# Attention head pairs with two block products between their transposes and the last blocks in one PSUM bank; final rows written in groups of 3, 1, 3, 1

## The chip, the cores and the metric

The kernel runs on one core of one Trainium2 chip. The metric is the device time of one execution in microseconds, the median of several runs: 2482.18 us before the change (three runs, 2481.7 to 2482.43). The engines are named as in the profile: PE is TensorE (PEld its weight loads), DVE is VectorE, ACT is ScalarE, POOL is GpSimd, SP is SyncE, which here only issues DMAs.

## What is computed

A two-layer encoder trunk in fp32 over 640 tokens: 512 frames of a new stream (the prompt) and 8 running streams of 16 frames each (the samples), with a model width of 1024. Cut to what matters:

```python
for l in range(DEPTH):                                    # DEPTH = 2
    x = x + 0.5 * swiglu(rmsnorm(x, norm_ffn1[l]), ...)   # width 2816
    z = rmsnorm(x, norm_mix[l]) @ w_in[l]                 # conv B | C | V | q | k | v | gates
    y_conv = B * causal_conv3(C * V)                      # 512 channels
    s = q @ k.T * 64 ** -0.5 + rel_bias[clipped distance] # 8 heads x 64, chunk-banded mask
    y_attn = softmax(s) @ v
    x = x + (sig(g_c) * (y_conv @ w_conv_out) + sig(g_a) * (y_attn @ w_attn_out)) @ w_o
    x = x + 0.5 * swiglu(rmsnorm(x, norm_ffn2[l]), ...)
y = rmsnorm(x, norm_final)                                # 640 x 1024
```

New keys, values and convolution states are outputs too. The change touches two places: the prompt's `softmax(s) @ v`, and the final norm.

## The kernel before

**Layout.** Activations lie transposed, with channels on the 128 partitions: `x[k]` is channels 128k to 128k+127 by 640 tokens. Weights stream from DRAM in slabs of 128 x 1024 (`raw`, loaded by SP at L245). Every fp32 operand is split in two parts (ACT casts the high part at L305, DVE subtracts for the low part at L310), and each product is three PE matmuls (high x high, high x low, low x high).

**Block products.** The large products use a seven-product scheme on halves of 320 tokens. `seven` (L818) is a generator: for one pair of output rows it issues seven products in the order 11, 21, N6, T5, T7, 22, T4, each in two steps of 6 matmuls of 128x320 (`block`, L386), so 14 steps to a pair of rows. Banks `ma` (11, N6, T7, T4), `mb` (21) and `mc` (T5, then 22) hold the sums. Between two products into the same bank an engine has to read the bank: after T5, ACT copies `mc` to `c` (L848) before 22 may go on accumulating there; after N6, ACT copies `ma` (L844) before T7; after T7, DVE adds `ma` and `c` (L249) before T4.

**Attention.** For the prompt the 8 heads go in 4 pairs. `scores(p)` makes q times k for 128-row blocks of queries and keys (`pss`) and reduces them on DVE (L1805); ACT takes exponentials (L1969) and scales the rows (L1816). `values(p)` transposes the weights block by block on PE (`ptp`, L1829). For key block j there are 4-j blocks of 128 for each of the two heads e, one PSUM bank for each j and e. Each bank is then copied to SBUF (`pt`, L1832), and the product with the values follows (`py`, L1843: 8 matmuls of 64 rows, two for each j, shown as 16 records), which ACT copies out (L1845). PE executes in the order of the code here (it alone is ordered by hand in this stage; DVE and ACT instructions are placed by a scheduler, with the copies at raised priority). Between these parts `fill(n)` lets PE do n steps of the running block products, so that the other engines have time to finish what PE needs next. Before the change a pair is: 14 transposes (j = 0 and 1), 3 steps, 6 transposes (j = 2 and 3), 2 steps, `py`, 5 steps; pairs 0 to 2 have the scores of the next pair and 4 more steps ahead. For pairs 0 to 2 this comes to: transposes, T5, half of T7, transposes, the other half of T7 and half of 22, `py`, half of 22, T4 and 11 of the next pair of rows. In pair 3 it is: transposes, 21 and half of N6, transposes, half of N6 and half of T5, `py`, and so on.

**Banks.** The transposes, scores and `py` share a pool of four PSUM banks (`att`) in turn, so a bank's new user waits until its last user has been read.

**The end.** `Final.all` (L2013 to L2066) adds the last part of the second FFN to `x` and applies the final norm, in two parts of the tokens: A (the first 384) and B (the last 256). While PE makes B's products, DVE multiplies A's rows by the norm factor `frr` (L2112), two of the eight `x[k]` at a time, and SP writes them to `yout` (L2113): rows 0-1, 2-3 and 4-5 behind B's rows 5, 6 and 7, and rows 6-7 after B's norm factors have been put on a diagonal (L488), while PE spreads them over the partitions (`nbcf`, L2103). Then DVE scales B's eight rows (L2116), and SP and ACT in turn write each as a DMA of 128 KB (L2118).

Of the kernel before, what the change touches and what calls it, by code (L numbers as in the profile page):

```python
# [13 lines left out]
ALU = mybir.AluOpType  # L14
PSUM = bass.MemoryType.PSUM

P = 128
# [30 lines left out]
PARTS = slice(0, 3 * P), slice(3 * P, T)  # L48
# [132 lines left out]
def trunk(ctx: ExitStack, tc: tile.TileContext, xin, xtok, wst, small, pbias, samplebias, kcache, vcache,  # L181
          yout, ko, vo, co):
    nc = tc.nc
    PE, DVE, ACT, POOL, SP = nc.tensor, nc.vector, nc.scalar, nc.gpsimd, nc.sync
# [21 lines left out]
    def acc(name):  # L206
        return banks["acc"].tile([P, 2, 512], F32, tag="acc", name=name)

    def att(name):
        return banks["att"].tile([P, 512], F32, tag="att", name=name)  # L210
# [15 lines left out]
    for kind, inside in kinds():  # L226
        n = len(fourth)
# [20 lines left out]
    def add(out, a, b):  # L248
        DVE.tensor_tensor(out=out, in0=a, in1=b, op=ALU.add)  # L249
# [58 lines left out]
    def flush():  # L308
        for lo, src, hi in pending:
            DVE.tensor_tensor(out=lo, in0=src, in1=hi.bitcast(F32), op=ALU.subtract)  # L310
        pending.clear()
# [3 lines left out]
    def slab(hold=False):  # L315

        flush()
        i = used[0]
        used[0] += 1
        while len(ready) < min(i + 2, len(slabs)):  # L320
            prep(len(ready))
            flush()
        prep(i + 2)
        if not hold:
            flush()
        return ready[i], slabs[i]
# [19 lines left out]
    class Tiles:  # L346
# [6 lines left out]
        def take(self):  # L353
            if self.at == self.n:
                self.cur, (kind, _, width) = slab(hold[0])
                assert kind == "plain"
                self.at, self.n = 0, width // P
            j = self.at
            self.at += 1
            return tuple(c[:, j * P : (j + 1) * P] for c in self.cur)  # L360
# [4 lines left out]
    def soon():  # L365
        return tc.high_priority(offset=300)
# [42 lines left out]
    def stir(ps, n):  # L409
        for _ in range(n):  # L410
            PE.matmul(ps[:, :P], ones, ones, start=True, stop=True)
# [4 lines left out]
    xall = xp.tile([P, KT, T], F32, name="x")  # L416
# [48 lines left out]
    class Stats:  # L465
# [19 lines left out]
        def turn(self, out, r):  # L485

            n = out.shape[1] // P
            DVE.tensor_tensor(out=out.rearrange("p (c t) -> p c t", c=n),  # L488
                              in0=ident.unsqueeze(1).to_broadcast([P, n, P]),
                              in1=r.unsqueeze(2).to_broadcast([P, n, P]), op=ALU.mult)  # L490

    def scaled(out, ps, rr):
        DVE.tensor_tensor(out=halves(out), in0=two(ps), in1=halves(rr), op=ALU.mult)
# [121 lines left out]
    def opening(fp, name, goff, n, put, tails):  # L615
# [45 lines left out]
        def out(i):  # L661

            j, up = divmod(i, 2)
            if not up:
                gs.append(tmp(f"g{name}_{j}"))
                if j:
                    scaled(gs[j], ps[i], ex.rho)
                    ACT.activation(gs[j], gs[j], AF.Silu)
                else:
                    ACT.copy(halves(gs[j]), two(ps[i]))  # L670
                return
            u = tmp(f"u{name}_{j}") if j > 1 else fp.tile([P, T], F32, tag="cap", name=f"u{name}_{j}", bufs=5)
            us.append(u)
            if j:
                scaled(u, ps[i], ex.rho)
                DVE.tensor_tensor(out=u, in0=u, in1=gs[j], op=ALU.mult)
            else:
                ACT.copy(halves(u), two(ps[i]))
# [559 lines left out]
    def mixer(l, after):  # L1238
        with tc.tile_pool(name=f"yp{l}", bufs=1, reuse_waits="tile") as yp, \
# [19 lines left out]
            with tc.tile_pool(name=f"mp{l}", bufs=2, reuse_waits="tile") as mp:  # L1259
# [63 lines left out]
                with tc.manual_schedule(engines={mybir.EngineType.PE}):  # L1323
                    attention(l, h, st, stats, ops, mp, yas, ycp, both, others())
# [374 lines left out]
    def attention(l, h, norms, stats, ops, mp, yas, ycp, both, others):  # L1699


        rr = norms.rr
        npair = H // 2
        nt = T // P
        NQ = SEQ // P
# [30 lines left out]
        def fill(n):  # L1736
            for _ in range(n):
                next(stream, None)
# [80 lines left out]
        def values(p):  # L1819

            pt = [mp.tile([P, offs[-1] + SEQ], F32, name=f"pt{l}_{2 * p + e}", tag="pt") for e in range(2)]
            at = [sum(P * (NQ - i) for i in range(j)) for j in range(NQ)]

            def turn(j, e):
                w = (NQ - j) * P
                s = weights[2 * p + e]
                ptp = att(f"ptp{l}_{2 * p + e}_{j}")[:, :w]
                for i in range(j, NQ):
                    PE.transpose(ptp[:, (i - j) * P : (i - j + 1) * P],  # L1829
                                 s[:, offs[i] + j * P : offs[i] + (j + 1) * P], ident)  # L1830
                with soon():
                    (ACT.copy if e and j % 2 else DVE.tensor_copy)(pt[e][:, at[j] : at[j] + w], ptp)  # L1832

            for j in range(NQ):
                for e in range(2):
                    turn(j, e)
                if j % 2:
                    yield
            py = att(f"py{l}_{p}")
            for j in range(NQ):  # L1840
                for e in range(2):
                    hh = 2 * p + e
                    PE.matmul(py[e * HD : (e + 1) * HD, j * P :], vs[j][:, hh * HD : (hh + 1) * HD],  # L1843
                              pt[e][:, at[j] : at[j] + (NQ - j) * P], start=j == 0, stop=j == NQ - 1)
            ACT.copy(yas[:, p, 0:SEQ], py)  # L1845
            yield
# [5 lines left out]
        for p in range(npair):  # L1852
            if p + 1 < npair:
                scores(p + 1)
                fill(4)
            vals = values(p)
            next(vals)
            fill(3)
            next(vals)
            fill(2)  # L1860
            next(vals)
            fill(5)


        sbias = mp.tile([P, KS], F32, name=f"sbias{l}", bufs=1)
# [143 lines left out]
    class Final:  # L2009
# [8 lines left out]
        def all(self, ops):  # L2018
            ws = [[tiles.take() for _ in ops] for m in range(KT)]
            flush()  # L2020
            rr = pool[0].tile([P, PARTS[0].stop], F32, tag="even", name="frr", bufs=1)
            A, B = PARTS

            ACT.activation(early, x[KT - 1][:, 0:1], AF.Sqrt, bias=epst[:, 0:1], scale=0.0)
            for m in range(KT):
                self.product(0, m, ops, ws[m])
                self.take(0, m, m < KT - 1)
                if m:
                    self.scale(m - 1)
            for m in range(KT):  # L2030
                self.product(1, m, ops, ws[m])
                if m == 2:
                    self.ps = att("npsf0")[:, : A.stop // P]
                    for b in range(A.stop // P):
                        PE.matmul(self.ps[:, b : b + 1], self.ssum[0][:, b * P : (b + 1) * P], ones[:, 0:1],
                                  start=True, stop=True)
                    self.root(0)
                if m == 3:
                    self.turn(0)
                    self.scale(KT - 1)  # L2040
                if m == 4:
                    ps = self.spread(0)
                if m == 5:
                    self.ps = acc("npsf1")[:, :, 0]
                    self.idle = acc("stirf")[:, 0]
                    self.add(self.ssum[1], True)
                if m > 4:
                    self.add(self.sq)
                if m == 0:
                    last = self.sq  # L2050
                self.take(1, m, m < 4)
                if m == 0:
                    add(self.ssum[0], self.ssum[0], last)
                if m == 4:
                    ACT.copy(rr, ps)
                if m > 4:
                    self.two(2 * m - 10, rr)
            stir(self.idle, 3)
            self.add(self.sq, False, True)
            stir(self.idle, 5)  # L2060
            self.root(1)
            self.turn(1)
            self.two(6, rr)
            ps = self.spread(1)
            for k in range(KT):
                self.out(k, B, ps)  # L2066
# [40 lines left out]
            xk = x[k][:, PARTS[0]]  # L2107
            ACT.activation(xk, xk, AF.Copy, scale=sm[:, O_GF + k : O_GF + k + 1])

        def two(self, k, rr):  # L2110
            z = xall[:, k : k + 2, PARTS[0]]
            DVE.tensor_tensor(out=z, in0=z, in1=rr.unsqueeze(1).to_broadcast([P, 2, rr.shape[1]]), op=ALU.mult)  # L2112
            SP.dma_start(yout[:, k : k + 2, PARTS[0]], z)  # L2113

        def out(self, k, c, ps):
            DVE.scalar_tensor_tensor(out=x[k][:, c], in0=x[k][:, c], scalar=sm[:, O_GF + k : O_GF + k + 1],  # L2116
# [167 lines left out]
```

## Time and profile before

| | |
|---|---|
| median of three runs | 2482.18 us |
| the profiled execution's own time | 2482.18 us |
| its span, first to last instruction | 2480.2 us |
| mean granted TensorE clock | 0.999 |
| PE busy | 2469.0 us |
| DVE busy | 2119.5 us |
| ACT busy | 1442.9 us |
| POOL busy | 361.1 us |
| DMA, mean over the span | 125 GB/s |

All times in the rows are microseconds from the start of the span. A row of the timeline has the start, the duration, the engine, the line, the operation, the tiles (out<-in), the shape and a count of merged instructions; in square brackets stands how long the engine was idle before it and what released it. The profiled execution took 1.98 us more than its span, and its time is that of the median run.

### The profile page before, as it was taken

Reading aid. Unit: us, or ns where it says so; the run is one execution under the profiler, and the core shown is the slowest. Engines: PE = TensorE matmul, PEld = TensorE weight load, DVE = VectorE, ACT = ScalarE, POOL = GpSimd, SP = SyncE. Lnnn points to the kernel's source line nnn. Section 1 sums busy time; section 2 is a strip of 40 time slices with the busy share of each in tenths; the row PEclk is TensorE's granted clock in tenths of the full one; section 3 lists DMA queues with packets and bytes.
Section 4 is the critical chain, followed back from the end, with each engine's and each line's share of the span. In section 5 each row is a group of like instructions: output and inputs, shape, how many; then the busy total and the mean of one; then the engine's idle time right before and its main releaser. Section 6 shows DMA issues by size and latency. Waiting matters only on the chain.

```text
span 2480.2 us, 43569 instructions
## 1 busy us (share of the span) xinstructions
PE 2469.0 (100%) x17070; PEld 2422.0 (98%) x17070; DVE 2119.5 (85%) x3344; ACT 1442.9 (58%) x2337; POOL 361.1 (15%) x445
## 2 busy tenths in 40 slices
PE   9999999999999999999999999999999999999998
PEld 9999999889999999999999999998899999999998
DVE  7789888878888899888798889888788888989887
ACT  6445556665666555555565555556656665555555
POOL 0011211210111011111001111221101210111111
PEclk9999999999999999999999999999999999999999
DMA  5245665335345345555435454643344553555554
GB/s 189 82 115 125 136 136 130 107 111 175 104 112 153 95 117 121 133 136 136 117 92 129 129 132 123 138 120 110 122 156 123 119 140 92 122 131 124 129 136 111
DMA packets 134925, 310.72 MB, mean 125 GB/s; under 512 B 12896, under 2 KB 76768, under 8 KB 134720
## 3 DMA queue, kind: packets, MB, share of 16 engines
q1 hardware_dynamic: 70640, 221.80, 27.2%
q0 software_dynamic: 63360, 85.50, 20.7%
q8 instruction: 133, 2.18, 0.4%
q10 hardware_dynamic: 720, 0.65, 0.1%
q14 instruction: 72, 0.59, 0.1%
HBM read 223.75 MB, written 7.94 MB: 93 GB/s over the span
## 4 chain that ended last, share of the span: by engine, by line
PE 96%; ACT 2%; DVE 1%; DMA 0%; issue 0%; DVEq 0%
PE pab L395 12%; PE paa L395 11%; PE pcb L395 6%; PE pca L395 6%; PE dab L1086 5%; PE daa L1086 5%; PE qa L395 4%; PE po L372 4%; PE pbb L395 3%; PE pba L395 3%; PE dcb L1086 3%; PE dca L1086 3%; PE pda L372 2%; PE pv L1752 2%; PE poa L372 2%; PE ma_cv L395 2%
## 5 line engine op out<-in xcount | busy, mean ns | idle before, releaser
L310 DVE TENSOR_TENSOR wlo<-raw,whi 128x1024 fp32r<-128x1024 f32 (+1 forms) x582 | 597.4, 1030 | 243.2 <-ACT whi L305 240.1
L305 ACT CAST whi<-raw 128x1024 fp32r<-128x1024 f32 (+1 forms) x582 | 520.3, 896 | 359.2 <-PE pbb L395 39.4
L305 ACT CAST whi<-s 128x1024 fp32r<-128x1024 f32 (+1 forms) x164 | 153.4, 936 | 243.9 <-issue 109.1
L395 PE MATMUL pab<-xhib,whi 128*128 128x320 f32 x704 | 217.8, 309 | 0.0
L395 PE MATMUL pab<-xlob,whi 128*128 128x320 f32 x704 | 217.4, 309 | 0.0
L395 PE MATMUL pab<-xhib,wlo 128*128 128x320 f32 x704 | 217.4, 309 | 0.0
L395 PE MATMUL paa<-xhia,whi 128*128 128x320 f32 x640 | 197.9, 309 | 0.0
L395 PE MATMUL paa<-xhia,wlo 128*128 128x320 f32 x640 | 197.7, 309 | 0.0
L395 PE MATMUL paa<-xloa,whi 128*128 128x320 f32 x640 | 197.7, 309 | 0.0
L310 DVE TENSOR_TENSOR wlo<-s,whi 128x1024 fp32r<-128x1024 f32 (+1 forms) x164 | 176.3, 1075 | 6.4 <-ACT whi L305 6.1
L395 PEld LDWEIGHTS pab<-xhib,whi 128*128 128x128 f32 x704 | 132.2, 188 | 0.2
L395 PEld LDWEIGHTS pab<-xlob,whi 128*128 128x128 f32 x704 | 132.2, 188 | 0.2
L395 PEld LDWEIGHTS pab<-xhib,wlo 128*128 128x128 f32 x704 | 132.2, 188 | 0.0
L395 PEld LDWEIGHTS paa<-xloa,whi 128*128 128x128 f32 x640 | 120.2, 188 | 0.1
L395 PEld LDWEIGHTS paa<-xhia,whi 128*128 128x128 f32 x640 | 120.2, 188 | 0.1
L395 PEld LDWEIGHTS paa<-xhia,wlo 128*128 128x128 f32 x640 | 120.2, 188 | 0.0
L249 DVE TENSOR_TENSOR raw<-raw,raw 128x512 f32<-128x512 f32 x164 | 112.0, 683 | 1.2
L249 DVE TENSOR_TENSOR raw<-s,raw 128x512 f32<-128x512 f32 x164 | 111.9, 682 | 0.0
L395 PE MATMUL pcb<-xhib,whi 128*128 128x320 f32 x352 | 108.9, 309 | 0.0
L395 PE MATMUL pcb<-xlob,whi 128*128 128x320 f32 x352 | 108.7, 309 | 0.0
L395 PE MATMUL pcb<-xhib,wlo 128*128 128x320 f32 x352 | 108.7, 309 | 0.0
L1110 POOL DMA_DIRECT2D x<-c_b x52 | 62.6, 1203 | 310.4 <-ACT c_b L1103 104.1
(852 smaller groups left out, 8144.9 us busy)
## 6 DMA issues: line engine op xcount, KB each, us to landing
raw<-in_wst SPq DMA_DIRECT2D x374, 512.0 KB, 3.6
x<-c_b POOLq DMA_DIRECT2D x52, 320.0 KB, 5.1
x<-c_a POOLq DMA_DIRECT2D x50, 320.0 KB, 5.0
kc<-in_kcache SPq DMA_DIRECT2D x32, 256.0 KB, 3.7
vc<-in_vcache SPq DMA_DIRECT2D x16, 512.0 KB, 5.5
ub<-cbb POOLq DMA_DIRECT2D x42, 160.0 KB, 5.9
ua<-cba POOLq DMA_DIRECT2D x38, 160.0 KB, 5.5
x<-u_a POOLq DMA_DIRECT2D x18, 320.0 KB, 5.1
```

The lines of the kernel that those rows point to most:

```text
L249: DVE.tensor_tensor(out=out, in0=a, in1=b, op=ALU.add)
L305: ACT.copy(hi[:, d], src[:, c])
L310: DVE.tensor_tensor(out=lo, in0=src, in1=hi.bitcast(F32), op=ALU.subtract)
L372: PE.matmul(ps[a] if isinstance(ps, list) else ps[:, a, :HT], w, x[:, a * HT : (a + 1) * HT], start=first and j == 0, stop=last and j == 2)
L395: PE.matmul(ps, a, b, start=start and kp == 0 and j == 0, stop=stop and kp == NP - 1 and j == 2, skip_group_check=True)
L1086: PE.matmul(ps[u], w, y, start=start and i == 0 and j == 0, stop=i == 1 and j == 2, skip_group_check=True)
L1110: POOL.dma_start(rows(r, cols), z, accum_op=ALU.add)
L1752: PE.matmul(pv[t], xx[:, t * P : (t + 1) * P], w[:, kk * AW : (kk + 1) * AW], start=c == 0 and kk == 0 and j == 0, stop=c == KT // 2 - 1 a ...
```

## The change

In `values(p)`: one bank still takes one j and e for j = 0, 1 and 2, but for j = 3 the single blocks of both heads share one bank. Of the copies from the banks, DVE now takes j = 0 and 1 of both heads, and j = 2 and 3 of the first; ACT takes j = 2 and 3 of the second (before: j = 1 and 3 of the second). The steps around them go from 3, 2, 5 to 2, 2, 6, the same sum: for pairs 0 to 2 the order is now transposes, T5, transposes, T7, `py`, 22, T4, 11; for pair 3 transposes, 21, transposes, N6, `py`, T5. In `Final`, A's rows are scaled and written as 0-2, 3, 4-6 and 7.

```diff
             for j in range(NQ):
+                ptps = [att(f"ptp{l}_{2 * p + e}_{j}") for e in range(2 if j < NQ - 1 else 1)]
+                if j == NQ - 1:
+                    ptps = [ptps[0][:, e * P : (e + 1) * P] for e in range(2)]
                 for e in range(2):
-                    turn(j, e)
+                    turn(ptps[e], j, e)
+                    if j < NQ - 1:
+                        take(ptps[e], j, e)
+                if j == NQ - 1:
+                    for e in range(2):
+                        take(ptps[e], j, e)
                 if j % 2:
                     yield
...
+            def take(ptp, j, e):
+                w = (NQ - j) * P
                 with soon():
-                    (ACT.copy if e and j % 2 else DVE.tensor_copy)(pt[e][:, at[j] : at[j] + w], ptp)
+                    (ACT.copy if e and j > 1 else DVE.tensor_copy)(pt[e][:, at[j] : at[j] + w], ptp[:, :w])
...
             next(vals)
-            fill(3)
+            fill(2)
             next(vals)
             fill(2)
             next(vals)
-            fill(5)
+            fill(6)
...
                 if m > 4:
-                    self.two(2 * m - 10, rr)
+                    self.rows(*((0, 3), (3, 1), (4, 3))[m - 5], rr)
...
             self.turn(1)
-            self.two(6, rr)
+            self.rows(7, 1, rr)
...
-        def two(self, k, rr):
-            z = xall[:, k : k + 2, PARTS[0]]
-            DVE.tensor_tensor(out=z, in0=z, in1=rr.unsqueeze(1).to_broadcast([P, 2, rr.shape[1]]), op=ALU.mult)
-            SP.dma_start(yout[:, k : k + 2, PARTS[0]], z)
+        def rows(self, k, n, rr):
+            z = xall[:, k : k + n, PARTS[0]]
+            DVE.tensor_tensor(out=z, in0=z, in1=rr.unsqueeze(1).to_broadcast([P, n, rr.shape[1]]), op=ALU.mult)
+            SP.dma_start(yout[:, k : k + n, PARTS[0]], z)
```

What this does to the order of the instructions, at three places. The first is PE in layer 0, pair 0, around `py`. Names end in a number of the tile; `ma_qk_5261<-thi` is product T7 and `mc_qk_5382<-hhim` or `<-hlom` product 22. Before:

```order
L395 MATMUL ma_qk_5261<-thi_3_4696,whi_5257 128x320
L395 MATMUL ma_qk_5261<-tlo_3_4697,whi_5257 128x320
L395 MATMUL ma_qk_5261<-thi_3_4696,wlo_5258 128x320
L395 MATMUL mc_qk_5382<-hhim_1_4635,whi_5257 128x320
L395 MATMUL mc_qk_5382<-hlom_1_4636,whi_5257 128x320
L395 MATMUL mc_qk_5382<-hhim_1_4635,wlo_5258 128x320
L395 MATMUL mc_qk_5382<-hhim_3_4643,whi_5257 128x320
L395 MATMUL mc_qk_5382<-hlom_3_4644,whi_5257 128x320
L395 MATMUL mc_qk_5382<-hhim_3_4643,wlo_5258 128x320
L1843 MATMUL py_0_5436<-pt_0_5357,v_0_4887 64x512
L1843 MATMUL py_0_5436<-pt_1_5358,v_0_4887 64x512
L1843 MATMUL py_0_5436<-pt_0_5357,v_1_4888 64x384
```

And after (lines behind the edit in `values` stand 9 further down, so L1852 is what L1843 was):

```order
L395 MATMUL ma_qk_5261<-thi_3_4696,whi_5257 128x320
L395 MATMUL ma_qk_5261<-tlo_3_4697,whi_5257 128x320
L395 MATMUL ma_qk_5261<-thi_3_4696,wlo_5258 128x320
L1852 MATMUL py_0_5427<-pt_0_5357,v_0_4887 64x512
L1852 MATMUL py_0_5427<-pt_1_5358,v_0_4887 64x512
L1852 MATMUL py_0_5427<-pt_0_5357,v_1_4888 64x384
L1852 MATMUL py_0_5427<-pt_1_5358,v_1_4888 64x384
L1852 MATMUL py_0_5427<-pt_0_5357,v_2_4889 64x256
L1852 MATMUL py_0_5427<-pt_1_5358,v_2_4889 64x256
L1852 MATMUL py_0_5427<-pt_0_5357,v_3_4890 64x128
L1852 MATMUL py_0_5427<-pt_1_5358,v_3_4890 64x128
L395 MATMUL mc_qk_5382<-hhim_1_4635,whi_5257 128x320
```

Before, half of T7 and the first half of 22 (which begins with the `mc_qk` rows shown) stood between the last transposes and `py`; now the whole of T7 stands there, and the whole of 22 behind `py`.

The second place is ACT in the same pair. L844 copies `ma` after N6, L848 copies `mc` after T5, L305 casts a slab of weights, L1969 and L1816 belong to the softmax of the next head, and L1832 copies banks of transposes. Before:

```order
L844 COPY capsm_4687<-ma_qk_5261 128x320
L1969 ACTIVATE s_3_5282,st_3_5283<-s_3_5282,st_3_5283 128x128
L1969 ACTIVATE s_3_5282,st_3_5283<-s_3_5282,st_3_5283 128x256
L1832 COPY pt_1_5358<-ptp_1_1_5376 128x384
L1816 ACTIVATE s_2_5277<-s_2_5277,st_2_5278 128x128
L1816 ACTIVATE s_2_5277<-s_2_5277,st_2_5278 128x256
L1816 ACTIVATE s_2_5277<-s_2_5277,st_2_5278 128x384
L305 CAST whi_5398<-raw_5396 128x1024
L848 COPY c_4698<-mc_qk_5382 128x320
L1816 ACTIVATE s_2_5277<-s_2_5277,st_2_5278 128x512
L1832 COPY pt_1_5358<-ptp_1_3_5419 128x128
```

And after (L1978 is what L1969 was; `ptp_0_3_5403` is the bank that both heads share for j = 3):

```order
L844 COPY capsm_4687<-ma_qk_5261 128x320
L1978 ACTIVATE s_3_5282,st_3_5283<-s_3_5282,st_3_5283 128x128
L1978 ACTIVATE s_3_5282,st_3_5283<-s_3_5282,st_3_5283 128x256
L1816 ACTIVATE s_2_5277<-s_2_5277,st_2_5278 128x128
L1816 ACTIVATE s_2_5277<-s_2_5277,st_2_5278 128x256
L1816 ACTIVATE s_2_5277<-s_2_5277,st_2_5278 128x384
L1816 ACTIVATE s_2_5277<-s_2_5277,st_2_5278 128x512
L848 COPY c_4698<-mc_qk_5382 128x320
L305 CAST whi_5411<-raw_5409 128x1024
L1833 COPY pt_1_5358<-ptp_1_2_5396 128x256
L1833 COPY pt_1_5358<-ptp_0_3_5403 128x128
```

The copy of 384 is gone from ACT, a copy of 256 has come behind the cast, and the copy of `mc` (L848), which stood right behind the cast of 1024, now stands right ahead of it. In the same stretch DVE now has all its copies of the pair (512, 512, 384, 384, 256 and 128 columns) ahead of its subtraction for that slab (L310), where its copies for j = 2 and 3 stood behind it. In each layer SP issues one weight slab (`raw`, L245) behind the two loads of the value cache (`vc`) of samples 0 and 1 instead of ahead of them. POOL's order is the same.

The third place is DVE at the end of the program. L2078 adds B's products to `x`, L2112 scales A's rows, L2098 and L488 make B's norm factors, L2116 scales B's rows. Before:

```order
L2078 SCALAR_TENSOR_TENSOR x<-pdf_5_27190,x 128x256
L2112 TENSOR_TENSOR x<-x,frr 128x2x384
L2078 SCALAR_TENSOR_TENSOR x<-pdf_6_27208,x 128x256
L2112 TENSOR_TENSOR x<-x,frr 128x2x384
L2078 SCALAR_TENSOR_TENSOR x<-pdf_7_27222,x 128x256
L2112 TENSOR_TENSOR x<-x,frr 128x2x384
L2098 RECIPROCAL ninvf<-nrmsf 128x2
L488 TENSOR_TENSOR fsum_27031<-ident,ninvf 128x256
L2112 TENSOR_TENSOR x<-x,frr 128x2x384
L2116 SCALAR_TENSOR_TENSOR x<-x,sm,nbcf_27251 128x256 x8
```

And after (numbers of lines 9 higher):

```order
L2087 SCALAR_TENSOR_TENSOR x<-pdf_5_27182,x 128x256
L2121 TENSOR_TENSOR x<-x,frr 128x3x384
L2087 SCALAR_TENSOR_TENSOR x<-pdf_6_27200,x 128x256
L2121 TENSOR_TENSOR x<-x,frr 128x384
L2087 SCALAR_TENSOR_TENSOR x<-pdf_7_27214,x 128x256
L2121 TENSOR_TENSOR x<-x,frr 128x3x384
L2107 RECIPROCAL ninvf<-nrmsf 128x2
L488 TENSOR_TENSOR fsum_27023<-ident,ninvf 128x256
L2121 TENSOR_TENSOR x<-x,frr 128x384
L2125 SCALAR_TENSOR_TENSOR x<-x,sm,nbcf_27243 128x256 x8
```

The order is the same; the four scalings now take 3, 1, 3 and 1 rows of `x` instead of 2 each. The rest of the program is unchanged.

More of the change, by code (lines that the diff above doesn't have):

```diff
@@ L1822, in values, with turn @@
             at = [sum(P * (NQ - i) for i in range(j)) for j in range(NQ)]
-            def turn(j, e):
-                w = (NQ - j) * P
+            def turn(ptp, j, e):
                 s = weights[2 * p + e]
-                ptp = att(f"ptp{l}_{2 * p + e}_{j}")[:, :w]
                 for i in range(j, NQ):
```

## The prediction

> **What bounds the kernel now.** I read the page first. Its head and the list of engines:
>
> ```profile
> span 2480.2 us, 43569 instructions
> PE 2469.0 (100%) x17070; PEld 2422.0 (98%) x17070; DVE 2119.5 (85%) x3344; ACT 1442.9 (58%) x2337; POOL 361.1 (15%) x445
> ```
>
> PE leaves 11.2 us of 2480.2 unused, and part of that is the end, when only the output is still moving. Neither part of the change takes work from PE, so it can gain in two ways only: where PE stands still, or behind PE's last matmul. Who makes PE stand still is in the waits of PE; the columns are the waiter, the engine waited for, total us, times and the longest:
>
> ```profile
> PE mc_qk L395 <- ACT c L848: 1.6, 4, 0.4
> ...
> PE mc_cv L395 <- ACT c L848: 0.8, 2, 0.4
> ```
>
> Six waits, one line: the first matmul of product 22 waits until ACT has copied `mc` after T5. By their places they are pairs 0, 1 and 2 of both layers; pair 3 has none. I went to the first in the timeline of PE:
>
> ```profile
> 494.64 0.31 PE L395 MATMUL ma_qk<-thi,whi 128*128 128x320 f32 x1
> ...
> 495.53 0.82 PE L1829 MATMUL ptp<-ident,yc 128*128 128x128 f32 x6
> 496.10 0.40 PE L395 MATMUL ma_qk<-thi,whi 128*128 128x320 f32 x1
> ...
> 496.92 0.31 PE L395 MATMUL ma_qk<-thi,wlo 128*128 128x320 f32 x1
> 497.63 0.42 PE L395 MATMUL mc_qk<-hhim,whi 128*128 128x320 f32 x1 [0.40 <-ACT c L848]
> 497.89 0.31 PE L395 MATMUL mc_qk<-hlom,whi 128*128 128x320 f32 x1
> ...
> 498.71 2.38 PE L1843 MATMUL py<-pt,v 128*64 128x512 f32 x16
> 501.01 0.42 PE L395 MATMUL mc_qk<-hhim,whi 128*128 128x320 f32 x1
> ```
>
> Ends are modelled and overlap, so I count from start to start. Six matmuls of T7 take 495.53 - 494.64 = 0.89 us, 0.148 each. From T7's last matmul (496.92) to the second of 22 (497.89) are 0.97 us where two steps, 0.30, would do: **0.67 us lost**, not the 0.40 in the bracket. The last of the six:
>
> ```profile
> 1764.78 0.31 PE L395 MATMUL ma_cv<-thi,wlo 128*128 128x320 f32 x1
> 1765.52 0.41 PE L395 MATMUL mc_cv<-hhim,whi 128*128 128x320 f32 x1 [0.43 <-ACT c L848]
> 1765.77 0.30 PE L395 MATMUL mc_cv<-hlom,whi 128*128 128x320 f32 x1
> ```
>
> 0.99 - 0.30 = 0.69 us. Six by 0.68 are **4.1 us**. By the waits' own totals, 1.6 + 0.8, they are 2.4 us, which I keep as the lower end. Why the copy is late stands in ACT's timeline:
>
> ```profile
> 494.65 0.46 ACT L1832 COPY pt<-ptp 128x384 f32<-128x384 f32 x1
> 495.01 1.31 ACT L1816 ACTIVATE s<-s,st 128x128 f32<-128x128 f32 x3
> 496.22 1.04 ACT L305 CAST whi<-raw 128x1024 fp32r<-128x1024 f32 x1
> 497.16 0.42 ACT L848 COPY c<-mc_qk 128x320 f32<-128x320 f32 x1
> 497.47 0.73 ACT L1816 ACTIVATE s<-s,st 128x512 f32<-128x512 f32 x1
> 498.10 0.25 ACT L1832 COPY pt<-ptp 128x128 f32<-128x128 f32 x1
> ```
>
> No row waits: ACT is a queue here, and the copy stands behind a copy of 384, three scalings and a cast.
>
> **The pairs, step by step.** *PE.* The transposes, T7 and `py` change places; the numbers of matmuls and of passages from one kind to another are the same, so the work costs nothing more. After: six transposes from 494.64 take 496.10 - 495.53 = 0.57, to 495.21. T7 whole is 0.97 (496.10 to 496.92 and one step) and 0.89, to 497.07. `py` takes 501.01 - 498.71 = 2.30, to 499.37, and only then comes 22: 2.3 us later than the 497.07 at which it wanted to start.
>
> *ACT.* The 384 copy goes (0.36 from start to start). From 494.65: three scalings 1.21, the scaling of 512, which now stands ahead, 0.63, to 496.49; then the copy of `mc`, 0.42, done at 496.91. 22 wants it at 499.37: 2.5 us to spare. The six waits go: **-4.1 us**. Either half would have done in pair 0: with ACT's old order, `c` at 497.58 is still ahead of 499.37.
>
> *What is late next.* First, the banks. The last transposes start 0.89 us earlier and reuse the banks of the first ones. DVE's rows there:
>
> ```profile
> 492.81 0.68 DVE L1832 COPY pt<-ptp 128x512 f32<-128x512 f32 x1
> 493.58 0.18 DVE L1972 RECIPROCAL st<-st 128x4 f32<-128x4 f32 x1
> 493.68 1.12 DVE L1832 COPY pt<-ptp 128x512 f32<-128x512 f32 x2
> 497.30 1.23 DVE L310 TENSOR_TENSOR wlo<-raw,whi 128x1024 fp32r<-128x1024 f32 x1 [2.50 <-ACT whi L305]
> ```
>
> The first bank has been read at 493.49 and the next two at 494.80. The shared bank for j = 3 reuses the third, and PE comes to it after four transposes, at 494.64 + 4 x 0.095 = 495.02: 0.2 us to spare. Second, `py`. DVE has 2.5 us idle ahead of its subtraction, where its further copies now go (384, 256, 128; net 128 columns more than before), so `py` finds them. Of head 1, j = 2 comes from ACT: behind `c` (done 496.91; ACT goes on at about 496.80, since 497.16 to 497.47 is 0.31) the cast takes 0.94, to 497.74, the 256 copy at most the 384's 0.46, to 498.20. `py` reaches j = 2 after 1792 of 2560 columns, 497.07 + 0.70 x 2.30 = 498.68: 0.5 us to spare.
>
> A third point is the bank shared for j = 3: the transposes of both heads have to be in before either copy, and DVE's and ACT's copies go one after the other, one ACT row of 0.25 later. `py` reads j = 3 last, after 90% of its columns, so I cost it at nothing. The Trainium skill ("PSUM — Partial Sum Buffer", "PSUM bank collisions raise a hardware error") says that two engines, two readers among them, may not be on one bank and partitions at once, and that this must be guarded by bank; no run here shows it. By that rule both copies would be kept apart even though they read other columns, and it speaks against the shared bank; the sum stays as it is, as it is made with the copies apart.
>
> *SP.* Its one moved load stands behind two loads of the value cache. In layer 0 SP's row with the issue, and ACT's with the first use:
>
> ```profile
> 550.73 0.33 SPq L245 DMA_DIRECT2D raw<-in_wst  x1
> ```
>
> ```profile
> 570.27 1.05 ACT L305 CAST whi<-raw 128x1024 fp32r<-128x1024 f32 x1 [1.18 <-PE mc_b L395]
> ```
>
> 19.5 us lie between them, so a few us later cost nothing; without this cover PE would wait for that slab, by what the issue comes later.
>
> **The end.** DVE's rows there, of which the last eight are B's:
>
> ```profile
> 2467.46 0.95 DVE L2112 TENSOR_TENSOR x<-x,frr 128x768 f32<-128x768 f32 x1
> 2468.73 0.42 DVE L2078 SCALAR_TENSOR_TENSOR x<-pdf,x 128x256 f32<-128x256 f32 x1 [0.32 <-PE pdf L2073]
> ...
> 2470.27 0.95 DVE L2112 TENSOR_TENSOR x<-x,frr 128x768 f32<-128x768 f32 x1
> 2471.86 0.17 DVE L2098 RECIPROCAL ninvf<-nrmsf 128x2 f32<-128x2 f32 x1 [0.64 <-ACT nrmsf L2093]
> ...
> 2472.40 0.95 DVE L2112 TENSOR_TENSOR x<-x,frr 128x768 f32<-128x768 f32 x1
> 2473.28 3.22 DVE L2116 SCALAR_TENSOR_TENSOR x<-x,sm,nbcf 128x256 f32<-128x256 f32 x8
> ```
>
> 256 columns take 0.42 and 768 take 0.95, so 384 take some 0.55 and 1152 some 1.35. Three rows from 2467.46 end at 2468.81, 0.08 behind the add that PE releases at 2468.73; three from 2470.27 end at 2471.62, ahead of the reciprocal at 2471.86. The chain to B's scaling is not longer, and the 0.08 goes in the second scaling, which is 0.40 shorter. I leave the start of B's scaling (2473.28) where it is. What moves is the bytes. The DMA rate over 2468 to 2480 in 40 slices of 0.3 us:
>
> ```profile
> GB/s 0 0 0 0 164 358 384 353 51 5 348 374 364 225 343 364 379 220 0 0 0 333 343 399 338 341 341 324 355 335 341 352 335 331 324 14 0 0 0 0
> ```
>
> The first data move half way into slice 4, at 2469.36, 0.95 us after the scaling's end (2468.41). From slice 21 (2474.30) to 2478.51 the DMA engines run without a gap at some 342 GB/s: 0.39 MB of rows 6 and 7 and 1.05 MB of B. Three empty slices (18 to 20) lie ahead of this burst. After the change rows 4 to 6 (0.59 MB) are scaled at 2471.62 and move from 2472.57 to 2474.30; row 7 (0.20 MB, 0.58 us) follows to 2474.88, then B, 8 x 0.384 = 3.07, to 2477.95. No earlier than this can it be by much: B's last scaling ends at 2476.50, and 0.95 + 0.38 behind it is 2477.83. So 2478.51 becomes some 2477.9: **-0.6 us**, at most 0.7, at least 0.4 if the handover from row 7 leaves a gap.
>
> The Trainium skill ("DMA: Bandwidth & Descriptors", "Bandwidth") wants DMAs batched to 1 MiB or more, which speaks against writing smaller pieces last; if each piece cost its 2.0 us besides its bytes in turn, as an estimate from that page the eight pieces of B would take over 16 us. The burst above took 4.2 us with all its pieces, so they overlap and the row decides.
>
> **Sum.** -4.1 - 0.6 = -4.7 us. The profiled execution took 2482.18 us, which is the median of the runs too, so the time after is **2477.5 us**. A measurement of this kernel can tell about 0.2% from no change, 5 us or 2477.2: the forecast lies just inside.
>
> **The rivals.**
> - *The end gives nothing*: the new pieces move later than reckoned, or the burst is set by B's own pace (one 0.40 us scaling for each piece of 0.38). Against it: the three empty slices. Then -4.1: 2478.1.
> - *A new wait takes half of the gain in the pairs*: `py` waits for ACT's 256 copy behind the cast. It decides when that copy is over 0.5 us late, and 0.8 us late costs 0.3 of the 0.68. For it: ACT has no idle row in the stretch; against: 0.5 us to spare. Then -2.0 - 0.6: some 2479.6.
> - *The six waits vanish and PE stands still later for the same time*, as another engine sets the pace. Against it: DVE had 2.5 us idle there, and PE's list of waits names no one else in these stages. Then only the end stays: 2481.6.
> - *Slower*: the last transposes wait for their bank. The four first copies are now DVE's alone, in series, and if a subtraction of 1.23 us gets ahead of them (by a late cast), the 0.2 us to spare are gone; from there each 0.1 us is lost six times. With the whole 1.23 it is 1.03 x 6 = 6.2 us: 2477.5 + 6.2 = 2483.7. Against it: DVE's order has the copies ahead of that subtraction.
>
> **How the numbers follow.** Forecast 70% (around 2477.5, half of it on each side of the bound of 2477.2, which lies that near); the end gives nothing 11%; half the gain 11%; given back 5%; slower 3%. The range is 2476.6 to 2479.6: downward for a larger loss per wait than start to start shows (0.1 us each) and the 0.1 of the end, upward through the second and third case and the 2.4 us of the waits' own totals. Faster by over 0.2%: half of the forecast's share, 35%; within 0.2%: 63%; slower by over 0.2% (above 2487) only if the bank's wait grows beyond that price: 2%.
>
> **What would show it.** Right: no PE wait on `c` L848; ACT has it ahead of the cast; the passage from T7 to `py` takes no longer than two steps; the last burst has no three empty slices ahead and ends near 2473.8 with PE's end 4.1 earlier. Wrong: PE rows that wait for `pt` ahead of `py` or for a bank ahead of `ptp`, or rows elsewhere that wait for `raw`, `whi` or `wlo`.

## The result, and the profile after

The changed kernel takes 2478.86 us (median of 22 runs, 2478.37 to 2480.03) where the kernel before took 2482.21 in the same series: 3.35 us less, a ratio of 0.9987 with a 95% interval of 0.9981 to 0.9993. The forecast was 2477.5 in a range of 2476.6 to 2479.6. The sign and the range hold; of the 4.7 us forecast, 1.35 are missing. The profiled execution took 2479.38 us with a span of 2476.7; the run at the median has a span of 2476.8, so the profile shows an ordinary execution and only its time outside the span is long. The head of the page after:

```profile
span 2476.7 us, 43563 instructions
PE 2469.1 (100%) x17070; PEld 2422.7 (98%) x17070; DVE 2121.1 (86%) x3344; ACT 1441.0 (58%) x2337; POOL 361.2 (15%) x445
```

The span is 3.5 us shorter with PE's busy time unchanged, so what went is idle time. PE's waits after, the whole list:

```profile
PE stira L411 <- POOL ones L404: 1.1, 1, 1.1
```

The six waits for `c` are gone, and by this list PE waits nowhere but at the start. The first pair shows how, PE first (L1852 is `py`, L1833 the copies):

```profile
496.81 0.30 PE L395 MATMUL ma_qk<-thi,wlo 128*128 128x320 f32 x1
497.05 2.37 PE L1852 MATMUL py<-pt,v 128*64 128x512 f32 x16
499.35 0.42 PE L395 MATMUL mc_qk<-hhim,whi 128*128 128x320 f32 x1
```

and ACT:

```profile
494.55 1.91 ACT L1816 ACTIVATE s<-s,st 128x128 f32<-128x128 f32 x4
496.37 0.40 ACT L848 COPY c<-mc_qk 128x320 f32<-128x320 f32 x1
496.67 1.05 ACT L305 CAST whi<-raw 128x1024 fp32r<-128x1024 f32 x1
497.62 0.53 ACT L1833 COPY pt<-ptp 128x256 f32<-128x256 f32 x2
```

`py` starts at 497.05 (reckoned: 497.07) and 22 at 499.35 (499.37); `c` is done at 496.77 (496.91), and the 256 copy no later than 498.15, ahead of the 498.68 at which `py` wants it. Pair 0 went as reckoned. At the end of the program, DVE and the DMA rate over 2464.5 to 2476.5 in slices of 0.3 us:

```profile
2467.54 1.35 DVE L2121 TENSOR_TENSOR x<-x,frr 128x1152 f32<-128x1152 f32 x1
...
2469.67 0.55 DVE L2121 TENSOR_TENSOR x<-x,frr 128x384 f32<-128x384 f32 x1
2470.54 3.22 DVE L2125 SCALAR_TENSOR_TENSOR x<-x,sm,nbcf 128x256 f32<-128x256 f32 x8 [0.32 <-PE nbcf L2112]
```

```profile
GB/s 0 0 0 0 0 0 0 0 123 384 379 358 384 358 379 256 0 36 358 364 384 353 389 353 374 331 331 342 345 345 328 338 342 345 341 120 0 0 0 0
```

1152 columns take 1.35 and 384 take 0.55, as estimated, and the last burst starts in slice 17 behind one empty slice instead of three.

So the missing 1.35 us are on PE, in waits too short for the list. They show in the sums of PE's steps (a step is the time from the start of one matmul to the start of the next), sorted by what follows what (us, against before; each profile has all 17,070 matmuls). The first row is product to product (1473.6 before), the second the 160 transposes with the steps into and out of them (18.5), the third `py` (16.8), the fourth the step from a product to the next scores (1.9):

| | after | e1 | e3 | e4 | e5 | e6 | e8 | e9 | e10 |
|---|---|---|---|---|---|---|---|---|---|
| products | -3.6 | -3.7 | -4.0 | -4.0 | -2.7 | -3.6 | -4.0 | -3.6 | -4.0 |
| transposes | +0.7 | +0.8 | 0 | +1.4 | 0 | +1.8 | +4.7 | 0 | 0 |
| `py` | 0 | 0 | +3.8 | 0 | 0 | 0 | 0 | 0 | 0 |
| next scores | +0.2 | +0.2 | 0 | 0 | 0 | 0 | 0 | +0.4 | 0 |
| sum | -2.7 | -2.7 | -0.1 | -2.5 | -2.7 | -1.8 | +0.7 | -3.2 | -4.0 |
| time against before | -3.35 | -2.66 | -1.00 | -3.38 | -3.47 | -2.55 | -0.25 | -3.90 | -4.77 |

The other columns are the experiments below; e1 has the old end, all others there the new one. With 0.7 us for the new end taken off the sum, every column gives its time within 0.3 us. The steps that are not in the table differ from profile to profile: in a second profile of the changed kernel they sum to 0.5 us more than in the first. I lean on this table where the times alone can't decide: the 95% intervals of the ratios are about 0.0009 wide on each side, 2 us, while the runs of one kernel lie mostly within 0.6 us of their median. The intervals of e2, e3 and e8 include a ratio of 1.

**Where the after column lost.** In pairs 1 and 2 the last transposes are late. Pair 1, PE:

```profile
514.20 1.06 PE L1827 MATMUL ptp<-ident,s 128*128 128x128 f32 x6
515.02 0.40 PE L395 MATMUL ma_qk<-thi,whi 128*128 128x320 f32 x1
```

and DVE:

```profile
512.95 0.18 DVE L1981 RECIPROCAL st<-st 128x4 f32<-128x4 f32 x1 [0.62 <-ACT yc L1978]
513.05 1.72 DVE L1833 COPY pt<-ptp 128x512 f32<-128x512 f32 x3
```

Six transposes take 0.82 us where pair 0 needs 0.57. The fifth should start at 514.64 (four steps of 0.109) but needs the bank of DVE's third copy, which ends at 513.05 + 1.72 = 514.77; the records have it at 514.82. Here a reciprocal of the next head's softmax stands ahead of DVE's first copy and waits 0.62 us for ACT; in pair 0 it stands behind the first copy. The first transposes begin at 491.25 and 510.91, so the third copy ends 3.45 us behind them in pair 0 (at 494.70) and 3.86 in pair 1. Pairs 1 and 2 of the two layers lose 0.25, 0.13, 0.24 and 0.12 us.

The order of the reciprocal is not new. Before the change, pair 1 had on DVE:

```profile
513.22 0.18 DVE L1972 RECIPROCAL st<-st 128x4 f32<-128x4 f32 x1 [0.63 <-ACT yc L1969]
513.31 1.72 DVE L1832 COPY pt<-ptp 128x512 f32<-128x512 f32 x3
```

There the first transpose started at 511.58 and the third copy ended at 515.03, 3.45 us behind it, just as in pair 0. What changed is who is early: with the wait of pair 0 gone, PE starts pair 1's transposes 0.67 us earlier (510.91), but DVE, whose reciprocal waits for ACT, ends the third copy only 0.26 us earlier (514.77). The 0.41 us between them are more than the 0.28 that pair 0 has to spare. No run moved the reciprocal, so that it is what holds DVE back is read from this row and not tested.

Ahead of pair 1's scores, PE:

```profile
504.59 0.31 PE L395 MATMUL ma_qk<-hhim,wlo 128*128 128x320 f32 x1
504.93 0.38 PE L1799 MATMUL pss<-k,q 64*128 64x128 f32 x2
```

and DVE:

```profile
504.39 0.48 DVE L1273 SCALAR_TENSOR_TENSOR k<-ma_qk,rrm 128x320 f32<-128x320 f32 x1
```

The step is 0.34 us, elsewhere 0.24: the keys are ready at 504.87, hardly earlier than before (504.91), and PE, 0.68 us earlier than before, is now there first. And at one later product in layer 0, PE and ACT:

```profile
616.63 0.31 PE L395 MATMUL ma_b<-thi,wlo 128*128 128x320 f32 x1
616.97 0.42 PE L395 MATMUL mc_b<-hhim,whi 128*128 128x320 f32 x1
```

```profile
615.41 1.05 ACT L305 CAST whi<-raw 128x1024 fp32r<-128x1024 f32 x1 [0.49 <-PE mc_b L395]
616.49 0.43 ACT L848 COPY c<-mc_b 128x320 f32<-128x320 f32 x1
```

Here a wait for `c` is new: with the slow second step behind it (0.25 us instead of 0.147) it costs 0.3 us.

### The profile page after: what moved, and what is told of

Read it like the earlier page. It is cut to its first block, busy times and chain, and to the rows that moved or that the text cites. A ratio compares the mean times of both kernels' runs of the same rounds, so it can differ in the third digit from the quotient of the medians.

```text
span 2476.7 us, 43563 instructions
## 1 busy us (share of the span) xinstructions
PE 2469.1 (100%) x17070; PEld 2422.7 (98%) x17070; DVE 2121.1 (86%) x3344; ACT 1441.0 (58%) x2337; POOL 361.2 (15%) x445
## 4 chain that ended last, share of the span: by engine, by line
PE 99%; DMA 0%; DVE 0%; SPq 0%; issue 0%; DVEq 0%
PE pab L395 13%; PE paa L395 11%; PE pcb L395 6%; PE pca L395 6%; PE dab L1086 5%; PE daa L1086 5%; PE qa L395 4%; PE po L372 4%; PE pbb L395 3%; PE pba L395 3%; PE dcb L1086 3%; PE dca L1086 3%; PE ma_cv L395 2%; PE ma_qk L395 2%; PE pda L372 2%; PE pv L1752 2%
## 5 line engine op out<-in xcount | busy, mean ns | idle before, releaser
L310 DVE TENSOR_TENSOR wlo<-raw,whi 128x1024 fp32r<-128x1024 f32 (+1 forms) x582 | 598.2, 1031 | 237.7 <-ACT whi L305 235.2
L305 ACT CAST whi<-raw 128x1024 fp32r<-128x1024 f32 (+1 forms) x582 | 519.9, 897 | 358.0 <-PE pbb L395 39.4
L305 ACT CAST whi<-s 128x1024 fp32r<-128x1024 f32 (+1 forms) x164 | 153.5, 936 | 242.3 <-issue 109.4
L310 DVE TENSOR_TENSOR wlo<-s,whi 128x1024 fp32r<-128x1024 f32 (+1 forms) x164 | 176.6, 1077 | 7.4 <-ACT whi L305 6.9
```

Of the source, the lines that this page charges most:

```text
L305: ACT.copy(hi[:, d], src[:, c])
```

## The experiments

Each was timed in five rounds (11 runs) beside the kernel before. The interval is that of the ratio.

**e1, the pairs alone.** `self.rows(2 * m - 10, 2, rr)` and `self.rows(6, 2, rr)`: A's rows two at a time, as before.

> The new pairs with A's rows written two at a time as before. Theory: the two parts add up, and the profile after has PE end 2.7 us earlier than before and the rest of the gain (0.8 us) behind PE. So this kernel takes 2.7 us less than before (some 2479.5), with PE's last matmul as early as after the change, and the last output burst again with rows 6 and 7 in it, ending some 0.7 us later than after. Rival (the end's gain is only PE's gain passed on): the time is that of the changed kernel, 2478.9.

Measured: 2479.31, 2.66 less than before (0.9989, 0.9980 to 0.9998); PE's last matmul starts at 2470.18, after the change at 2470.12, and the last burst ends at 2475.8 instead of 2475.1.

**e2, the end alone.** `two` replaced by `rows` in the kernel before.

> The old pairs with A's rows written 3, 1, 3, 1. Theory: PE ends where it did, the span is 0.6 to 0.8 us shorter: some 2481.5. Rival: no gain without the earlier PE, 2482.2. The six waits for c stay.

Measured: 2481.29, 0.68 less (0.9997, 0.9988 to 1.0006); the six waits are there. The DMA rate over 2467 to 2479:

```profile
GB/s 0 0 0 0 0 0 0 0 102 374 364 364 379 379 353 302 5 5 343 379 358 379 364 374 369 324 345 338 352 331 331 345 348 338 342 154 0 0 0 0
```

The last burst starts at 2472.4 where it started at 2474.3 before, carries more, and ends at 2477.6 instead of 2478.5; of these 0.9 us, 0.2 are PE's, whose last matmuls come that much earlier in this profile. The parts add up: 2.66 + 0.68 = 3.34. The missing gain is in the pairs.

**e3, more ahead of the last transposes.**

```diff
-            fill(2)
+            fill(3)
             next(vals)
-            fill(2)
+            fill(1)
```

> The changed kernel with 3, 1 and 6 steps in place of 2, 2 and 6: half of T7 moves back ahead of the last transposes, py and 22 stay where they are. Theory: in pairs 1 and 2 of the profile after, the fifth of the last six transposes starts 0.12 to 0.25 us late since its bank is not yet read (0.73 us in all four); 0.89 us more ahead of it removes all four waits, and py comes no later, so the kernel takes 0.7 us less than the changed one: some 2478.1. Rival 1 (those steps hid a later wait, and py now waits for its j = 2 and 3 copies with half the time behind the last transposes): the same time or more, 2478.9 to 2480, with starts of py that are late. Rival 2 (the late transposes have another cause than the bank): they stay.

Measured: 2480.97, 1.00 less than before (0.9995, 0.9986 to 1.0004), so 2.3 us of the changed kernel's gain are lost. The late transposes did go, by the cause named; rival 1 came with a larger price than I gave it. Pair 1, PE, DVE and ACT:

```profile
517.48 3.08 PE L1852 MATMUL py<-pt,v 128*64 128x512 f32 x16
520.48 0.42 PE L395 MATMUL mc_qk<-hhim,whi 128*128 128x320 f32 x1
```

```profile
518.17 1.23 DVE L310 TENSOR_TENSOR wlo<-raw,whi 128x1024 fp32r<-128x1024 f32 x1 [1.48 <-ACT whi L305]
519.31 0.17 DVE L1981 RECIPROCAL st<-st 128x4 f32<-128x4 f32 x1
519.40 0.26 DVE L1833 COPY pt<-ptp 128x128 f32<-128x128 f32 x1
```

```profile
519.82 0.24 ACT L1833 COPY pt<-ptp 128x128 f32<-128x128 f32 x1
```

`py` takes 3.00 us from start to start instead of 2.30. The six matmuls that moved were also cover: with the transposes later, the scheduler put DVE's last copy behind a subtraction of 1.23 us (in the changed kernel it stands ahead), and ACT's copy of the same bank follows DVE's: DVE's ends at 519.66, ACT's starts at 519.82. In the changed kernel DVE's copy ends at 515.76, so this order costs nothing there; here `py` waits for both copies. The Trainium skill ("PSUM — Partial Sum Buffer", "PSUM bank collisions raise a hardware error") asks for two engines' reads of one bank to be kept apart like this.

**e4, the order of PE without the new split.** The old split, `ACT.copy if e and j % 2`, with the new steps and the shared bank.

> The changed kernel with the old split of the copies (ACT takes j = 1 and 3 of head 1), so that c stands behind the cast again: the new order of PE alone. Theory: either half removes the waits for c, since 22 comes 2.3 us later; none appears. The late transposes stay, 0.7 us in all, since DVE's third copy, which they wait for, is as late as with four copies on DVE (a reciprocal that waits for ACT stands ahead of the first). So the time of the changed kernel, 2478.9, within 0.3. Rival (they wait because DVE has four copies in series): they go, 2478.1. Second rival (ACT's order is what removes the waits for c): the six waits are back, 2483.

Measured: 2478.59, 3.38 less (0.9986, 0.9977 to 0.9995). ACT in pair 1:

```profile
514.44 0.46 ACT L1833 COPY pt<-ptp 128x384 f32<-128x384 f32 x1
...
515.91 1.04 ACT L305 CAST whi<-raw 128x1024 fp32r<-128x1024 f32 x1
516.85 0.43 ACT L848 COPY c<-mc_qk 128x320 f32<-128x320 f32 x1
```

The cast is ahead of `c` again, and no wait for `c` is left: the order of PE does it without the new split. The product column is even the full -4.0, and the waits ahead of the scores and at `mc_b` are absent. But the transposes cost 1.4, twice as much; PE:

```profile
514.24 1.15 PE L1827 MATMUL ptp<-ident,s 128*128 128x128 f32 x6
515.15 0.40 PE L395 MATMUL ma_qk<-thi,whi 128*128 128x320 f32 x1
```

My reason for expecting no difference was wrong: in this build the shared bank follows the bank that ACT copies (j = 1, head 1), read at 514.90, and the fifth transpose starts at 514.95. So the run doesn't decide on the rival, four copies in series on DVE. DVE's third copy was even in time here:

```profile
512.76 1.72 DVE L1833 COPY pt<-ptp 128x512 f32<-128x512 f32 x3
```

It ends at 514.48, ahead of the 514.68 at which the fifth transpose is due, but that transpose now needs another bank.

**e5, the split of the copies without the new order of PE.** The old `fill(3)`, `fill(2)`, `fill(5)`.

> The changed kernel with the old 3, 2 and 5 steps: the new split of the copies alone, with 22 again half ahead of py. c stands ahead of the cast on ACT. Theory: either half takes away most of the waits for c; c is done at 496.77 in pair 0 and 516.84 in pair 1 of the profile after, where 22 would now start at 497.05 and some 516.7, so 0 to 0.15 us is left of each wait. The late transposes go (-0.7 us). py begins 0.9 us later than in the kernel with 3, 1 and 6 steps, which covers the late j = 3 copies that cost that kernel 0.5 to 0.7 us in each of the first three pairs. So 0.2 to 0.7 us less than the changed kernel: 3.5 to 4.1 us less than before. Rival (only the order of PE takes the waits away): the six waits are back, and the time is 0.7 us below that of before.

Measured: 2478.67, 3.47 less (0.9986, 0.9977 to 0.9995). Pair 1, PE and ACT:

```profile
516.45 0.31 PE L395 MATMUL ma_qk<-thi,wlo 128*128 128x320 f32 x1
516.77 0.41 PE L395 MATMUL mc_qk<-hhim,whi 128*128 128x320 f32 x1
```

```profile
516.30 0.41 ACT L848 COPY c<-mc_qk 128x320 f32<-128x320 f32 x1
```

`c` is done at 516.71, and 22 starts at 516.77 instead of 516.60. Pair 0 has no wait, pairs 1 and 2 keep 0.28 and 0.34 us of the 0.68, in both layers. So the split, with the shared bank but without the new order of PE, takes 2.7 of 4.0 us.

**e6, a bank for each head again for j = 3.** `range(2)` for the banks, and no halves.

> The changed kernel with a bank for each head for j = 3, as before the change. Theory: the sixth of the last transposes now reuses the bank that DVE copies fourth, 0.47 us behind the third, where PE comes 0.11 us later: 0.36 us more in pairs 1 and 2, 0.1 in pair 0, in both layers, 1.6 us in all, so some 1.8 us less than before instead of 3.4. Rival (the shared bank costs, since its copies follow one another): the time falls below that of the changed kernel.

Measured: 2479.59, 2.55 less (0.9990, 0.9981 to 0.9999). Pair 1's transposes:

```profile
514.12 1.33 PE L1827 MATMUL ptp<-ident,s 128*128 128x128 f32 x6
515.21 0.39 PE L395 MATMUL ma_qk<-thi,whi 128*128 128x320 f32 x1
```

1.09 us instead of 0.82 and 0.57. The transposes cost 1.1 more than in the changed kernel (1.6 expected): the shared bank pays, because one bank fewer has to be read in time. The gain is 0.8 us smaller than the changed kernel's 3.35: these 1.1 us, less the 0.2 ahead of the scores, which are absent here.

**e8, less ahead of the last transposes.** `fill(1)`, `fill(3)`, `fill(6)`.

> The changed kernel with 1, 3 and 6 steps: the last transposes come 0.92 us earlier still. Theory (they wait for the third bank to be read, the point of the rival that ended slower): with the 0.28 us to spare in pair 0 and the waits of 0.25 and 0.13 in pairs 1 and 2, the fifth transpose is now 0.64, 1.17 and 1.05 us late, with 0 to 0.1 in pair 3: 2.9 us a layer where 0.4 was, so 5.0 us slower than the changed kernel and 1.6 us slower than before. Rival (the short waits are noise of that place): the same as the changed kernel.

Measured: 2481.89, 0.25 less than before (0.9999, 0.9991 to 1.0008), 3.1 slower than the changed kernel where I expected 5.0. PE's waits and pair 1:

```profile
PE ptp L1827 <- DVE pt L1833: 1.1, 6, 0.2
```

```profile
514.24 0.44 PE L1827 MATMUL ptp<-ident,s 128*128 128x128 f32 x2
514.83 0.90 PE L1827 MATMUL ptp<-ident,s 128*128 128x128 f32 x4 [0.16 <-DVE pt L1833]
515.49 0.39 PE L395 MATMUL mc_qk<-hhim,whi 128*128 128x320 f32 x1
```

The mechanism is the one named, and the list now sees it. Pair 0 loses 0.72 us (0.64 reckoned), but pairs 1 and 2 only 0.77 and 0.72 instead of 1.17 and 1.05: I had moved PE alone by 0.92 us, while the 0.7 lost in a pair give DVE and ACT a start on PE in the next. That is the reverse of what happens in the changed kernel.

**e9, two banks for the last six transposes.** Both heads share for j = 2 as well, so only the first two banks have to be read.

```diff
-                ptps = [att(f"ptp{l}_{2 * p + e}_{j}") for e in range(2 if j < NQ - 1 else 1)]
-                if j == NQ - 1:
-                    ptps = [ptps[0][:, e * P : (e + 1) * P] for e in range(2)]
+                ptps = [att(f"ptp{l}_{2 * p + e}_{j}") for e in range(2 if j < 2 else 1)]
+                if j > 1:
+                    w = (NQ - j) * P
+                    ptps = [ptps[0][:, e * w : (e + 1) * w] for e in range(2)]
```

> The changed kernel with j = 2 of both heads in one bank too, so that the last six transposes need only the first two banks read. Theory: the second bank is read 0.47 us ahead of the third and PE comes to it at the same place or 0 to 0.2 us later than it did to the third, so the late transposes of pairs 1 and 2 go: 0.7 us less than the changed kernel, 4.1 us less than before, with the order of the other instructions unchanged. Rival (ACT and DVE are slowed by the two banks that they share, or py waits): the same time or more.

Measured: 2478.24, 3.90 less (0.9985, 0.9976 to 0.9994). The late transposes are gone, all 0.7 us; but PE, earlier again, now waits ahead of pair 2's scores too, 0.1 us in each of four places. Ahead of pair 1's:

```profile
504.42 0.31 PE L395 MATMUL ma_qk<-hhim,wlo 128*128 128x320 f32 x1
504.76 0.49 PE L1799 MATMUL pss<-k,q 64*128 64x128 f32 x4
```

**e10, e9 with the old split.** What was clean in e4 and what was clean in e9.

> The changed kernel with both edits tried apart: the old split of the copies (ACT takes j = 1 and 3 of head 1, DVE j = 2 of both) and one bank for both heads for j = 2 as well as for j = 3. Theory: with the old split PE's matmuls of the block products and its first matmuls of the next scores lost nothing, and only the late transposes were left (1.4 us, waiting for ACT's copy of the fourth bank); with the last six transposes needing the first two banks alone, these go too. So 1.4 us less than the old split with one shared bank: 4.8 us less than before, the sum that was forecast for the change. Rival (py now waits for DVE's three copies in series, or the smaller waits only move on to the next scores, as with two banks and the new split): 3.4 to 4.2 us less than before.

Measured: 2477.18, 4.77 less than before (0.9980, 0.9972 to 0.9989), 1.69 less than the changed kernel on the same chip. Pair 1, PE:

```profile
513.95 0.82 PE L1827 MATMUL ptp<-ident,s 128*128 128x128 f32 x6
514.52 0.39 PE L395 MATMUL ma_qk<-thi,whi 128*128 128x320 f32 x1
```

0.57 us, no step in the stage is longer than in an undisturbed pair, and the gain is the 4.0 of the waits and 0.7 of the end, which is the sum that was forecast for the change. This version beats both kernels.

**The changed kernel once more**, on e10's chip.

> The changed kernel once more, on the same chip as the kernel with two shared banks and the old split: 3.3 us less than before; the waits of the profile after (late transposes of pairs 1 and 2, 0.1 us ahead of the scores of pair 1, 0.3 us ahead of one later product in layer 0) are all at the same places if they belong to the kernel, and elsewhere if they are chance.

Measured: 2478.87, 3.08 less (0.9986, 0.9977 to 0.9996). Its profile has the same waits at the same places (transposes +0.7, scores +0.2, 0.3 us at `mc_b`), so they belong to the kernel. One wait of 0.2 us for ACT (`aao`) stands in this profile's list alone.

## Why the prediction was right, and where it was short

- *PE bounds, and six waits for `c` are worth 4.1 us.* Right: 4.0 in e3, e4, e8 and e10. From the list's own totals it would have been 2.4.
- *Either half would do.* Right for PE's order (e4). For the split (e5) it holds in pair 0, the one I replayed; pairs 1 and 2 keep almost half.
- *What is late next, the banks: 0.2 us to spare.* This step failed. The number is right for pair 0 (third copy at 494.70, fifth transpose at 494.98), but I took it for all pairs. In pairs 1 and 2 PE comes earlier by what the pairs before have saved, and the copies follow only in part (0.67 against 0.26 us in pair 1), so the spare time is used up. The last transposes then wait for their bank, as in the slower rival, but not for its reason, a subtraction of 1.23 us ahead of the copies, and with 0.12 to 0.25 us in place of its 1.03. It cost 0.7 us (e9 takes it away, e8 enlarges it).
- *`py` finds its copies.* Right, with the 0.5 us to spare that was reckoned; e3 shows that this margin hangs on where the scheduler puts one copy.
- *PE's saved time is not given back.* Parts are, besides the 0.7 us of the banks: 0.2 us ahead of the scores, and some 0.4 in later products (0.3 at `mc_b`). The first goes with the old split: e4 and e10 have the cast ahead of `c`, and no such wait. I read it as the cast, and DVE's work behind it, coming later when `c` is ahead; no run changed that alone. The second is in all runs with the new split and 2, 2, 6 steps and in no other. The cast ahead of `c` begins 0.3 us later there, and why is open.
- *The shared bank and the moved load cost nothing.* The bank gains 1.1 us of waits (e6). No wait for the moved load is seen.
- *The end, -0.6.* 0.7 (e2, and e1 from the other side).
- *The range, up to 2479.6.* That the time lies in it is partly luck. Its upper part was reckoned for an end that gives nothing, for a wait of `py` and for smaller waits to begin with, and none of these came; what filled it are the new waits above, which the sum has at nothing.

## What to carry to other kernels

A margin replayed in the first iteration is not the margin of the next. The time that an engine saves brings it to the next iteration earlier, while the engines that it needs there follow only as far as their own chains let them (0.26 of 0.67 us here). So carry the saved time forward through each iteration, above all where the engine that must come first waits for a third; replaying the old rows of pair 1 alone would have shown the same 3.45 us as pair 0. Cover moved to one side of a step is taken from the other: three ways to place the same four steps around the last transposes (2 and 2, 3 and 1, 1 and 3) gave 2478.9, 2481.0 and 2481.9 us. Where waits are short, add up the steps from start to start by kind, since a list of waits by modelled ends can miss them: of the 3.8 us that e3 lost in `py` its list shows nothing.

## What the runs showed of the hardware

- After these waits the next step is slow too: the second matmul of 22 starts 0.25 us behind the first instead of 0.147, and the transpose behind a late one 0.166 instead of 0.109. Such a wait costs 0.06 to 0.1 us more than the wait. The same slow step stands behind `py` (499.35 to 499.60), where PE did not wait.
- The two heads' matmuls of `py`, on 64 columns of PE each, start 0.006 us apart and so go side by side (0.32 us from one pair of 384 columns to the next). Where the copies are late (e3, pair 1, j = 3) they don't: the two records of one head start at 519.71 and 519.87, those of the other at 520.12 and 520.28, behind ACT's copy.
